# Who makes the two parts of the third query block's weights: POOL alone, or POOL and VectorE

## The chip, the core and the metric

The kernel runs on one core of a Trainium2 chip. The metric is the device time of one execution in microseconds (us); three runs of the kernel before gave 1119.89, 1119.96 and 1120.11, median 1119.96. Every timeline below counts from the start of the profiled span.

## What is computed

An encoder trunk of two layers over 512 tokens of width 1024. Each layer adds a normalised mixer (token attention heads and memory cross-attention heads, then an output projection) and a normalised SwiGLU block. The change sits in the first layer's mixer, in the query projection:

```python
for i in range(DEPTH):
    h = rms_norm(x, g_mix_pre[i])
    proj = h @ w_in[i]
    q = proj[..., :Q_W].reshape(B, S, N_TOK_HEADS, HEAD_DIM)
    ...
    tok = mixer_a(q, k, v, attn_sink[i // N_MIXERS], cos_p, sin_p)
    mo = memory_attention(qm, km, vm)
    o = jnp.concatenate([tok, mo], axis=-1) @ w_o[i]
    x = x + rms_norm(o, g_mix_post[i])
```

`rms_norm(x, g)` multiplies by the vector `g_mix_pre`; the kernel folds that vector into the rows of the weights of the first mixer, so the weights are multiplied by it on their way to TensorE.

## The kernel before

All matrix products are made of 32-bit factors split into a high part `hi` (rounded to TensorE's fp32r format) and a low part `lo`, the remainder; each product is three matmuls, hi by hi, hi by lo, lo by hi (`mm3`, L273 to L275). So every weight block of 128x1024 has to be fetched into a tile `raw`, multiplied by the norm factor where there is one, and split into tiles `whi` and `wlo` before TensorE may use it. There are three `raw` tiles and four of each of `whi` and `wlo`, used in turn, and SP issues the transfers in program order: a transfer waits until the tile that it fills has been read by its last reader.

The first mixer works through a query block of four heads at a time, numbered c = 0 to 3 (c = 3 is the memory heads). Each query block has two weight blocks of 128x1024, z = 0 and 1. In the same stretch of time the mixer makes the keys and values of the memory, and starts the attention of the first heads:

- `prod` and `keys` of the memory (L388 to L427): ScalarE and VectorE take two accumulators in PSUM apart into `k2` and `vm` (L402, L404); POOL copies a part of `k2` (`again`, L414); TensorE turns `k2` twice (L421, L426), and VectorE copies the second result out (`kmb`, L427). The second turn uses one single PSUM bank.
- `score` (L557 to L586): TensorE multiplies queries and keys (L570, L571) into one of three PSUM banks used in turn, VectorE masks and takes the minimum (L576), ScalarE exponentiates (L582). Two of the three banks hold the memory's accumulators before.
- `normalise` (L611): VectorE makes the reciprocal `rd` (L618), POOL multiplies the four tiles `p` of a head by it (L621). `turn` (L624): TensorE transposes `p` (L631).

Who splits a weight block is set by a number per block in the table `PACE`: `qw[2 * c + z]`. It goes as `side` into `unit`, whose inner `part` handles half a block, in columns of 256 (`m`):

```python
            for k in range(c0 // m, c1 // m):
                c = slice(k * m, k * m + m)
                if side & 1:
                    nc.gpsimd.tensor_scalar(raw[:, c], raw[:, c], g[:, k:k + 1], 1.0, op0=OP.mult, op1=OP.mult)
                else:
                    self.split_scaled(hi[:, c], lo[:, c], raw[:, c], g[:, k:k + 1], side)
            if side & 1:
                self.split(hi[:, c0:c1], lo[:, c0:c1], raw[:, c0:c1], side)
```

With 3, POOL scales `raw` in place (L239, 256 columns each), makes `hi` by a multiplication by 1 (L281, 512 columns) and `lo` by a subtraction (L285, 512 columns). With 2, `split_scaled` is used: POOL makes `hi` as `raw` times the factor (L298, 256 columns), and VectorE makes `lo` as `raw` times the factor minus `hi` (L301, 256 columns). The multiplication on VectorE has two tensors in SBUF as sources.

The order on TensorE is written by hand, by times in the table `PACE`; on the other engines a scheduler at build time fixes one order for each, and at run time each engine takes its instructions in that order and waits at the head of its queue.

Of the kernel before, what the change touches and what calls it, by code (L numbers as in the profile page):

```python
# [34 lines left out]
URGENT = 150  # L35
LOTS = ((0, 8), (8, 14), (14, 22))

PACE = [{'lag': 1.692, 'vlag': 0.479, 'jstep': 0.213, 'kstep': 0.375, 'klag': 0.742, 'qoff': [0.212, 0.126, 0.099], 'qlag': 1.02, 'late': 0.6, 'moff': -0.235, 'mdur': 0.562, 'mlag': 0.697, 'kw': [0, 0, 2, 0], 'mw': [2, 1, 1, 0], 'qw': [1, 0, 0, 1, 3, 3, 3, 3], 'hoff': 0, 'ow': [10.3, 10.8, 12.2, 13.2], 'ox': 11.4, 'od': 0.3, 'hstep': 0.872, 'hlag': 1.742, 'hjstep': 0.135, 'hvlag': 0.751, 'owm': [0, 0, 0, 0, 0, 0, 0, 0], 'q0step': 0.27, 'q0off': -0.032, 'q0lag': 0.919, 'm0off': -0.078, 'm0dur': 0.002, 'm0lead': 1.887, 'mlead': 1.201, 'qlead': 0.921, 'q0lead': 1.555, 'qstep': 1.002, 'tw': [0, 0, 0, 0, 0, 0, 0, 0], 'h2off': 0}, {'lag': 1.824, 'vlag': 0.535, 'jstep': 0.218, 'kstep': 0.777, 'klag': 1.715, 'qoff': [-0.027, -0.162, -0.027], 'qlag': 1.189, 'late': 2.15, 'moff': -0.088, 'mdur': 0.384, 'mlag': 1.205, 'kw': [0, 0, 0, 0], 'mw': [0, 0, 0, 0], 'qw': [0, 0, 0, 0, 0, 3, 1, 1], 'hoff': 0, 'ow': [10.2, 10.7, 12.2, 13.2], 'ox': 11.3, 'od': 0.3, 'hstep': 0.946, 'hlag': 1.847, 'hjstep': 0.295, 'hvlag': 0.568, 'owm': [0, 0, 0, 0, 0, 0, 0, 0], 'q0step': 0.718, 'q0off': -0.018, 'q0lag': 1.136, 'm0off': -1.059, 'm0dur': 0.171, 'm0lead': 2.465, 'mlead': 3.162, 'qlead': 1.895, 'q0lead': 1.42, 'qstep': 0.998, 'tw': [0, 0, 0, 0, 0, 0, 0, 0], 'h2off': 0.016}]

# [141 lines left out]
class Trunk:  # L183
# [84 lines left out]
    def side(self, l, key, u):  # L268
        return PACE[l][key][u]

# [400 lines left out]
    def mixer(self, l, mkp, late, tokp):  # L671
        nc = self.nc
        pc = PACE[l]
        if l == 0:
# [619 lines left out]
```

## Time and profile before

| | us |
|---|---|
| median of 3 runs | 1119.96 |
| profiled execution, its own time | 1119.8 |
| its span | 1117.9 |
| TensorE busy | 1095.3 (98% of the span) |
| VectorE (DVE) busy | 838.8 |
| ScalarE (ACT) busy | 662.7 |
| GpSimd (POOL) busy | 202.9 |

The profiled execution lasted 1.9 us longer than its span, and lies 0.16 us below the median. In the rows below PE is TensorE's matmuls, PEld its weight loads, DVE VectorE, ACT ScalarE, POOL GpSimd, SP the engine that issues transfers. A row of a timeline gives start, duration, engine, line, operation, output and inputs, shape, count; in brackets stands how long the engine was idle before, and who ended it.

### The profile page before, as it was taken

How to read it: one execution, taken by the hardware profiler on the slowest of the kernel's cores; microseconds unless marked ns; L12 is line 12 of the kernel's file. 1: busy time of each engine (PE TensorE's matmuls, PEld its weight loads, DVE VectorE, ACT ScalarE, POOL GpSimd, SP SyncE). 2: the span in 40 equal slices, each digit the busy share in tenths (PEclk: the TensorE clock that was granted, in tenths of full speed). 3: DMA queues.
4: the chain of work that ended last, by engine and by line, in shares of the span. 5: the costliest groups of instructions: out<-in, count | busy, mean ns of one | idle time of the engine just before them, and what ended most of it. 6: DMA issues, size and time to landing. Idle time of an engine off the chain costs nothing.

```text
span 1117.9 us, 19566 instructions
## 1 busy us (share of the span) xinstructions
PE 1095.3 (98%) x7487; PEld 1005.7 (90%) x7487; DVE 838.8 (75%) x1401; ACT 662.7 (59%) x1349; POOL 202.9 (18%) x349
## 2 busy tenths in 40 slices
PE   9999999999999999999999999999999999999997
PEld 7889988999889989998898888878999899899986
DVE  5788886899547867885787988758996478669854
ACT  7578984766445544653467888756764256345631
POOL 5693331202000000000343553212000000000001
PEclk9999999999999999999999999999999999999999
DMA  6521025443753382326543221145137123422243
GB/s 238 192 81 50 20 77 188 151 151 116 247 177 108 110 291 76 100 79 209 163 167 114 77 76 39 38 157 183 47 105 226 58 81 113 147 68 98 84 167 113
DMA packets 38686, 139.30 MB, mean 125 GB/s; under 512 B 4416, under 2 KB 4800, under 8 KB 38464
## 3 DMA queue, kind: packets, MB, share of 16 engines
q1 hardware_dynamic: 38448, 137.91, 36.6%
q8 instruction: 59, 0.97, 0.4%
q14 instruction: 35, 0.29, 0.1%
q10 hardware_dynamic: 144, 0.14, 0.0%
HBM read 119.16 MB, written 18.87 MB: 123 GB/s over the span
## 4 chain that ended last, share of the span: by engine, by line
PE 67%; DVE 8%; ACT 3%; POOL 2%; issue 2%; DMA 0%; DVEq 0%; POOLq 0%; ACTq 0%
PE ps L1027 12%; PE ps L1028 11%; PE ps L1026 11%; PE ps L273 9%; PE ps L274 9%; PE ps L275 9%; PE tp L631 2%; PE o L646 1%; PE o L645 1%; DVE wlo L287 1%; DVE sf L287 1%; PE s L570 1%; PE s L571 1%; POOL r L307 1%; ACT junk L311 1%
## 5 line engine op out<-in xcount | busy, mean ns | idle before, releaser
L283 ACT ACTIVATE whi<-raw 128x1024 fp32r<-128x1024 f32 (+2 forms) x186 | 157.9, 863 | 177.9 <-PE ps L1028 78.5
L287 DVE TENSOR_TENSOR wlo<-raw,whi 128x1024 fp32r<-128x1024 f32 (+2 forms) x178 | 175.5, 996 | 74.8 <-ACT whi L283 68.9
L1027 PE MATMUL ps<-sf,wlo 128*128 128x256 f32 x640 | 179.7, 281 | 0.0
L1026 PE MATMUL ps<-sf,whi 128*128 128x256 f32 x640 | 179.7, 281 | 0.0
L1028 PE MATMUL ps<-sf,whi 128*128 128x256 f32 x640 | 179.7, 281 | 0.0
L273 PE MATMUL ps<-whi,f 128*128 128x512 f32 (+1 forms) x360 | 138.6, 385 | 0.0
L274 PE MATMUL ps<-wlo,f 128*128 128x512 f32 (+1 forms) x360 | 138.5, 385 | 0.0
L275 PE MATMUL ps<-whi,f 128*128 128x512 f32 (+1 forms) x360 | 138.4, 384 | 0.0
L1027 PE MATMUL ps<-a,wlo 128*128 128x256 f32 x480 | 134.0, 279 | 1.7 <-DVE wlo L287 1.7
L1026 PE MATMUL ps<-a,whi 128*128 128x256 f32 x480 | 134.4, 280 | 0.3 <-DVE c L1062 0.3
L1028 PE MATMUL ps<-a,whi 128*128 128x256 f32 x480 | 134.4, 280 | 0.0
L1027 PEld LDWEIGHTS ps<-sf,wlo 128*128 128x128 f32 x640 | 121.4, 190 | 0.5
L1026 PEld LDWEIGHTS ps<-sf,whi 128*128 128x128 f32 x640 | 121.1, 189 | 0.5
L1028 PEld LDWEIGHTS ps<-sf,whi 128*128 128x128 f32 x640 | 121.4, 190 | 0.0
L316 POOL TENSOR_SCALAR e<-sso 128x1 f32<-128x1 f32 x8 | 3.4, 422 | 565.5 <-ACT junk L311 565.3
L273 PE MATMUL ps<-whi,hT 128*128 128x256 f32 (+1 forms) x320 | 98.8, 309 | 0.0
L274 PE MATMUL ps<-wlo,hT 128*128 128x256 f32 (+1 forms) x320 | 94.0, 294 | 2.0 <-DVE wlo L287 1.4
L621 POOL TENSOR_SCALAR p<-p,rd 128x256 f32<-128x256 f32 (+2 forms) x128 | 76.9, 619 | 99.7 <-DVE rd L618 41.9
L275 PE MATMUL ps<-whi,hT 128*128 128x256 f32 (+1 forms) x320 | 93.7, 293 | 0.0
L1027 PEld LDWEIGHTS ps<-a,wlo 128*128 128x128 f32 x480 | 90.5, 188 | 2.3 <-DVE wlo L287 2.1
L1026 PEld LDWEIGHTS ps<-a,whi 128*128 128x128 f32 x480 | 90.4, 188 | 0.7 <-DVE c L1062 0.5
L1028 PEld LDWEIGHTS ps<-a,whi 128*128 128x128 f32 x480 | 90.1, 188 | 0.0
(205 smaller groups left out, 2740.3 us busy)
## 6 DMA issues: line engine op xcount, KB each, us to landing
raw<-in_wgu_dram SPq DMA_DIRECT2D x48, 512.0 KB, 4.2
raw<-in_wd_dram SPq DMA_DIRECT2D x44, 512.0 KB, 4.4
rb<-in_wgu_dram SPq DMA_DIRECT2D x40, 512.0 KB, 3.6
raw<-in_wo_dram SPq DMA_DIRECT2D x17, 512.0 KB, 3.6
raw<-in_wq_dram SPq DMA_DIRECT2D x16, 512.0 KB, 4.9
xt<-x SPq DMA_DIRECT2D x12, 512.0 KB, 4.4
raw<-in_wm_dram SPq DMA_DIRECT2D x8, 512.0 KB, 3.9
x<-y SPq DMA_DIRECT2D x8, 512.0 KB, 2.9
```

The costliest lines, as they stand in the source:

```text
L273: mm(out, lh, rh, start=first, stop=False)
L274: mm(out, lh, rl, start=False, stop=False)
L275: mm(out, ll, rh, start=False, stop=last)
L283: a = nc.scalar.activation(hi, src, AF.Copy)
L287: b = nc.vector.tensor_sub(lo, src, hi.bitcast(F32))
L307: g.tensor_tensor(r, r, self.mhalf[:, :r.shape[1]], op=OP.pow)
L311: self.nc.scalar.activation(scratch, x, AF.Square, scale=D ** -0.5, accum_out=ss)
L621: self.pooled = nc.gpsimd.tensor_scalar(hd["p"][z][:, :n], hd["p"][z][:, :n], rd[:, z:z + 1], 1.0, op0=OP.mult, op1=OP.mult)
L631: nc.tensor.transpose(tp[:, z], hd["p"][i][:, jj * P:(jj + 1) * P], self.ident)
L1026: mm(out, wh[:, s], rh, start=start and k == 0, stop=False, skip_group_check=True)
L1027: mm(out, wl[:, s], rh, start=False, stop=False, skip_group_check=True)
L1028: mm(out, wh[:, s], rl, start=False, stop=k == 3, skip_group_check=True)
```

## The change

Two entries of `qw` of the first layer go from 3 to 2, those of query block c = 2, z = 0 and 1. The table is one long line; the two entries are the fifth and sixth:

```diff
-PACE = [{... 'qw': [1, 0, 0, 1, 3, 3, 3, 3], ...
+PACE = [{... 'qw': [1, 0, 0, 1, 2, 2, 3, 3], ...
```

So for `raw_1073` (z = 0) and `raw_1128` (z = 1) the scaling in place, the copy and the subtraction on POOL go; POOL makes `hi` with the factor, VectorE `lo`. The blocks of c = 3, `raw_1579` and `raw_1615`, stay with POOL. The order of TensorE and of SP stays as it is.

POOL, from the split of block c = 1, z = 1 (`raw_705`) to the copy of the memory's second key tile (`k2_833`):

```order
 L285 TENSOR_TENSOR wlo_707<-raw_705,whi_706 128x512 x2
-L281 TENSOR_SCALAR whi_1074<-raw_1073 128x512 x2
-L285 TENSOR_TENSOR wlo_1075<-raw_1073,whi_1074 128x512 x2
-L239 TENSOR_SCALAR raw_1128<-raw_1128,cst_87 128x256 x3
+L298 TENSOR_SCALAR whi_1074<-raw_1073,cst_87 128x256 x4
 L414 TENSOR_SCALAR k2_808<-k2_808 128x4x64
-L239 TENSOR_SCALAR raw_1128<-raw_1128,cst_87 128x256
 L239 TENSOR_SCALAR raw_1579<-raw_1579,cst_87 128x256 x3
-L281 TENSOR_SCALAR whi_1129<-raw_1128 128x512 x2
+L298 TENSOR_SCALAR whi_1129<-raw_1128,cst_87 128x256 x4
 L414 TENSOR_SCALAR k2_833<-k2_833 128x4x64
```

Both before and after, three scalings of `raw_1579` stand ahead of the high part of `raw_1128`; now five instructions lie between the split of `raw_705` and them, where there were nine.

VectorE, from the rotary of the first query block's last tile (`qx_773`) to the memory's keys and values (`k2`, `vm`):

```order
 L437 TENSOR_TENSOR rt_775<-qx_773,cst_87 128x64
 L439 TENSOR_TENSOR qx_773<-qx_773,cst_87 128x4x16
+L301 SCALAR_TENSOR_TENSOR wlo_1075<-raw_1073,cst_87,whi_1074 128x256
 L440 TENSOR_TENSOR qx_773<-qx_773,rt_775 128x4x16
+L301 SCALAR_TENSOR_TENSOR wlo_1075<-raw_1073,cst_87,whi_1074 128x256 x2
 L287 TENSOR_TENSOR q2_791<-qx_773,q2_791 128x4x64
+L301 SCALAR_TENSOR_TENSOR wlo_1075<-raw_1073,cst_87,whi_1074 128x256
 L404 SCALAR_TENSOR_TENSOR k2_808<-ps_551,rs_114,k2_808 128x4x64
 L404 SCALAR_TENSOR_TENSOR vm_550<-ps_551,rs_114,vm_550 128x4x64
+L301 SCALAR_TENSOR_TENSOR wlo_1130<-raw_1128,cst_87,whi_1129 128x256 x3
 L404 SCALAR_TENSOR_TENSOR k2_833<-ps_558,rs_114,k2_833 128x4x64
 L404 SCALAR_TENSOR_TENSOR vm_550<-ps_558,rs_114,vm_550 128x4x64
```

Seven of the eight new subtractions stand ahead of the memory's second key tile, three of them directly ahead of it, and those three read `whi_1129`, which POOL makes.

VectorE, the rows that follow: the first head's masks (L576), the rotary of a tile of query block 1 (`qx_865`), and the copy of the memory's keys (`kmb`):

```order
 L437 TENSOR_TENSOR rt_867<-qx_865,cst_87 128x64
+L301 SCALAR_TENSOR_TENSOR wlo_1130<-raw_1128,cst_87,whi_1129 128x256
 L439 TENSOR_TENSOR qx_865<-qx_865,cst_87 128x4x16
-L440 TENSOR_TENSOR qx_865<-qx_865,rt_867 128x4x16
 L576 ISA p_889,nm_871<-s_886,mask_215,nsink_89 128x384
 L576 ISA nm_871 128x1
-L287 TENSOR_TENSOR q2_892<-qx_865,q2_892 128x4x64
+L440 TENSOR_TENSOR qx_865<-qx_865,rt_867 128x4x16
 L576 ISA p_904,nm_871<-s_901,mask_215,nsink_89 128x384
 L576 ISA nm_871 128x1
+L287 TENSOR_TENSOR q2_892<-qx_865,q2_892 128x4x64
 L427 CAST kmb_549<-tp_913 128x4x128
```

The eighth subtraction joins them, and two steps of the rotary come later; the copy of `kmb` keeps its place behind both masks.

## Rows read from the trace of the kernel before

**Rows 1.** Busy time of each engine, from the page.
```profile
PE 1095.3 (98%) x7487; PEld 1005.7 (90%) x7487; DVE 838.8 (75%) x1401; ACT 662.7 (59%) x1349; POOL 202.9 (18%) x349
```
**Rows 2.** Waits of PE between 40 and 112 us: total, times, longest.
```profile
PE tp L631 <- POOL p L621: 1.3, 2, 1.1
...
PE tp L426 <- DVE kmb L427: 0.3, 1, 0.3
```
**Rows 3.** Timeline of PE, 44 to 112 us.
```profile
65.75 0.45 PE L421 MATMUL tp<-identr,k 128*128 128x128 f32 x4
66.49 0.50 PE L426 MATMUL tp<-identr,k 128*128 128x128 f32 x4 [0.29 <-DVE kmb L427]
...
70.16 0.34 PE L571 MATMUL s<-kb,qT 128*128 128x384 f32 x1
71.56 0.33 PE L631 MATMUL tp<-cst,p 128*128 128x128 f32 x1 [1.06 <-POOL p L621]
72.12 0.33 PE L631 MATMUL tp<-cst,p 128*128 128x128 f32 x1 [0.23 <-POOL p L621]
72.21 0.36 PE L273 MATMUL ps<-whi,hT 128*128 128x256 f32 x1
```
**Rows 4.** Timeline of POOL, 20 to 110 us.
```profile
48.41 3.84 POOL L239 TENSOR_SCALAR raw<-raw,cst 128x256 f32<-128x256 f32 x8 [7.78 <-DMA raw<-in_wq_dram]
54.34 2.54 POOL L285 TENSOR_TENSOR wlo<-raw,whi 128x512 fp32r<-128x512 f32 x2 [2.09 <-ACT whi L283]
56.85 1.21 POOL L281 TENSOR_SCALAR whi<-raw 128x512 fp32r<-128x512 f32 x2
58.03 2.73 POOL L285 TENSOR_TENSOR wlo<-raw,whi 128x512 fp32r<-128x512 f32 x2
60.74 1.39 POOL L239 TENSOR_SCALAR raw<-raw,cst 128x256 f32<-128x256 f32 x3
...
68.53 2.36 POOL L239 TENSOR_SCALAR raw<-raw,cst 128x256 f32<-128x256 f32 x5
70.86 2.23 POOL L621 TENSOR_SCALAR p<-p,rd 128x256 f32<-128x256 f32 x4
```
**Rows 5.** SP's issues, 40 to 44 us; the first of them, us to landing.
```profile
40.66 2.01 SPq L227 DMA_DIRECT2D raw<-in_wq_dram  x2
raw<-in_wq_dram SPq DMA_DIRECT2D x1, 512.0 KB, 7.6
```
**Rows 6.** SP's issue between 56 and 59 us, and its time to landing.
```profile
56.91 0.33 SPq L227 DMA_DIRECT2D raw<-in_wq_dram  x1
raw<-in_wq_dram SPq DMA_DIRECT2D x1, 512.0 KB, 3.9
```
**Rows 7.** Timeline of DVE, 40 to 112 us.
```profile
52.57 1.69 DVE L301 SCALAR_TENSOR_TENSOR wlo<-raw,cst,whi 128x256 fp32r<-128x256 f32 x4 [0.67 <-ACT whi L300]
...
60.95 0.48 DVE L404 SCALAR_TENSOR_TENSOR k<-ps,rs,k 128x256 fp32r<-128x256 f32 x1 [0.56 <-ACT vm L402]
61.35 0.47 DVE L404 SCALAR_TENSOR_TENSOR vm<-ps,rs,vm 128x256 fp32r<-128x256 f32 x1
62.17 0.49 DVE L576 CUSTOM_DVE_ANT_0 p<-s,mask,nsink 128x256 f32<-128x256 f32 x1 [0.35 <-PE s L571]
...
65.66 0.68 DVE L427 CAST kmb<-tp 128x512 fp32r<-128x512 f32 x1
...
68.89 0.17 DVE L618 RECIPROCAL rd<-den 128x4 f32<-128x4 f32 x1
```
**Rows 8.** Four L301 beside POOL: timelines of DVE (26 to 40), POOL (20 to 110).
```profile
34.88 2.01 DVE L301 SCALAR_TENSOR_TENSOR wlo<-raw,cst,whi 128x256 fp32r<-128x256 f32 x4
35.38 2.12 POOL L239 TENSOR_SCALAR raw<-raw,cst 128x512 f32<-128x512 f32 x2 [1.09 <-DMA raw<-in_wm_dram]
```
**Rows 9.** Stretches at the end: engines' busy time, PEclk, DMA share, GB/s.
```profile
1111.00:1112.00 1.00, 0.00 (x0) 0.00 (x0) 0.81 (x2) 0.51 (x2) 0.00 (x0) 1.00 0.72 287
...
1115.00:1116.00 1.00, 0.00 (x0) 0.00 (x0) 0.00 (x0) 0.00 (x0) 0.00 (x0) 0.58 1.00 375
```

More of the change, by code (lines that the diff above doesn't have):

```diff
@@ L36 @@
 LOTS = ((0, 8), (8, 14), (14, 22))
-PACE = [{'lag': 1.692, 'vlag': 0.479, 'jstep': 0.213, 'kstep': 0.375, 'klag': 0.742, 'qoff': [0.212, 0.126, 0.099], 'qlag': 1.02, 'late': 0.6, 'moff': -0.235, 'mdur': 0.562, 'mlag': 0.697, 'kw': [0, 0, 2, 0], 'mw': [2, 1, 1, 0], 'qw': [1, 0, 0, 1, 3, 3, 3, 3], 'hoff': 0, 'ow': [10.3, 10.8, 12.2, 13.2], 'ox': 11.4, 'od': 0.3, 'hstep': 0.872, 'hlag': 1.742, 'hjstep': 0.135, 'hvlag': 0.751, 'owm': [0, 0, 0, 0, 0, 0, 0, 0], 'q0step': 0.27, 'q0off': -0.032, 'q0lag': 0.919, 'm0off': -0.078, 'm0dur': 0.002, 'm0lead': 1.887, 'mlead': 1.201, 'qlead': 0.921, 'q0lead': 1.555, 'qstep': 1.002, 'tw': [0, 0, 0, 0, 0, 0, 0, 0], 'h2off': 0}, {'lag': 1.824, 'vlag': 0.535, 'jstep': 0.218, 'kstep': 0.777, 'klag': 1.715, 'qoff': [-0.027, -0.162, -0.027], 'qlag': 1.189, 'late': 2.15, 'moff': -0.088, 'mdur': 0.384, 'mlag': 1.205, 'kw': [0, 0, 0, 0], 'mw': [0, 0, 0, 0], 'qw': [0, 0, 0, 0, 0, 3, 1, 1], 'hoff': 0, 'ow': [10.2, 10.7, 12.2, 13.2], 'ox': 11.3, 'od': 0.3, 'hstep': 0.946, 'hlag': 1.847, 'hjstep': 0.295, 'hvlag': 0.568, 'owm': [0, 0, 0, 0, 0, 0, 0, 0], 'q0step': 0.718, 'q0off': -0.018, 'q0lag': 1.136, 'm0off': -1.059, 'm0dur': 0.171, 'm0lead': 2.465, 'mlead': 3.162, 'qlead': 1.895, 'q0lead': 1.42, 'qstep': 0.998, 'tw': [0, 0, 0, 0, 0, 0, 0, 0], 'h2off': 0.016}]
@@ new lines @@
+PACE = [{'lag': 1.692, 'vlag': 0.479, 'jstep': 0.213, 'kstep': 0.375, 'klag': 0.742, 'qoff': [0.212, 0.126, 0.099], 'qlag': 1.02, 'late': 0.6, 'moff': -0.235, 'mdur': 0.562, 'mlag': 0.697, 'kw': [0, 0, 2, 0], 'mw': [2, 1, 1, 0], 'qw': [1, 0, 0, 1, 2, 2, 3, 3], 'hoff': 0, 'ow': [10.3, 10.8, 12.2, 13.2], 'ox': 11.4, 'od': 0.3, 'hstep': 0.872, 'hlag': 1.742, 'hjstep': 0.135, 'hvlag': 0.751, 'owm': [0, 0, 0, 0, 0, 0, 0, 0], 'q0step': 0.27, 'q0off': -0.032, 'q0lag': 0.919, 'm0off': -0.078, 'm0dur': 0.002, 'm0lead': 1.887, 'mlead': 1.201, 'qlead': 0.921, 'q0lead': 1.555, 'qstep': 1.002, 'tw': [0, 0, 0, 0, 0, 0, 0, 0], 'h2off': 0}, {'lag': 1.824, 'vlag': 0.535, 'jstep': 0.218, 'kstep': 0.777, 'klag': 1.715, 'qoff': [-0.027, -0.162, -0.027], 'qlag': 1.189, 'late': 2.15, 'moff': -0.088, 'mdur': 0.384, 'mlag': 1.205, 'kw': [0, 0, 0, 0], 'mw': [0, 0, 0, 0], 'qw': [0, 0, 0, 0, 0, 3, 1, 1], 'hoff': 0, 'ow': [10.2, 10.7, 12.2, 13.2], 'ox': 11.3, 'od': 0.3, 'hstep': 0.946, 'hlag': 1.847, 'hjstep': 0.295, 'hvlag': 0.568, 'owm': [0, 0, 0, 0, 0, 0, 0, 0], 'q0step': 0.718, 'q0off': -0.018, 'q0lag': 1.136, 'm0off': -1.059, 'm0dur': 0.171, 'm0lead': 2.465, 'mlead': 3.162, 'qlead': 1.895, 'q0lead': 1.42, 'qstep': 0.998, 'tw': [0, 0, 0, 0, 0, 0, 0, 0], 'h2off': 0.016}]
```

## The prediction

> **What bounds the kernel now.** I read the page's busy times first. TensorE is busy for 1095.3 of the 1117.9 us of the span, the other engines far less [rows 1]: time that TensorE gains or loses in the first mixer arrives at the end nearly one for one, and work that is taken from POOL or given to VectorE counts only where TensorE waits for it. So the second view is TensorE's waits in the stretch of the change, 40 to 112 us. Two of them matter. The largest is for POOL: 1.3 us, for the first head's scaled tiles `p` [rows 2]. The other is 0.3 us for VectorE's copy of `kmb` [rows 2].
>
> The third view is the timelines, for what lies behind each wait. TensorE multiplies the last scores at 70.16 and starts the transposes of `p` only at 71.56, held by POOL; the next product starts at 72.21 [rows 3]. VectorE had the reciprocal ready at 68.89 plus 0.17, that is at 69.06 [rows 7]; but POOL was scaling weights of block c = 3 until 70.89 and took up `p` at 70.86 [rows 4]. So POOL's queue of weights, not the softmax, is what TensorE waits for, and it is that queue which the change shortens. At `kmb`, VectorE is what comes last, 66.49 against a copy started at 65.66 [rows 3, 7]: this is a place where any delay of VectorE goes straight into TensorE.
>
> **What POOL sheds.** For one block before, POOL runs four scalings of 0.48 (3.84 for eight), two copies in 1.21 and two subtractions in 2.73 [rows 4]: 1.92 + 1.21 + 2.73 = 5.9 us. After, it makes four high parts of 256 columns. No such shape of L298 is in the stretch; L239 is the same operation with the same columns, so 0.48 each, 1.92 a block. POOL is relieved of about 4 us a block, 8 in all.
>
> **The gain.** With these 8 us gone POOL has nothing in front of `p` when the reciprocal comes, and TensorE's wait for `p` goes. At least it is the two stated waits, 1.06 + 0.23 = 1.29 us [rows 3]. At most it is all from the end of the scores, 70.16 + 0.34 = 70.50, to the next product at 72.21, 1.71 us [rows 3], as if the two transposes were hidden altogether. I take the middle, **1.5 us**.
>
> **The new wait.** VectorE gets eight L301. Alone four of them took 1.69, 0.42 each [rows 7]; four beside POOL took 2.01, 0.50 each [rows 8]. Were that all, 4 us of additional work would lie in VectorE's queue. But three of them stand directly in front of the memory's second L404, and need the high part of `raw_1128`. POOL makes that behind three scalings of `raw_1579`, and that tile is still on its way:
>
> - The transfer of `raw_1579` fills the tile that `raw_705` leaves. It is issued at 56.91, right after POOL's subtractions of 54.34 to 56.88 [rows 4, 6], which the change does not touch. It lands 3.9 later, at 60.81 [rows 6]. An earlier transfer was issued at 40.66, landed after 7.6, at 48.26, and POOL began at 48.41 [rows 4, 5], so 0.15 more: POOL begins at 60.96. Before, POOL had its own copies and subtractions until 60.74 [rows 4] and never saw this wait; now it is through with its four high parts (56.88 + 1.92 = 58.8) and a short copy, and stands idle for more than a us.
> - Three scalings, 1.39 [rows 4], to 62.35; the first high part, 0.48, at 62.83.
> - VectorE, which is through with its earlier work by about 61, waits there. Three L301 at 0.50, because POOL runs beside them: to 64.33. The L404 that ran at 60.95 [rows 7] runs 3.4 us late.
> - Two L404 at 0.40 (60.95 to 61.35) bring the first mask to 65.13, where it stood at 62.17 after an idle 0.35 [rows 7]: 2.96 late. From there to the copy of `kmb` the same work lies in front as before, plus the eighth L301, 0.50: 2.96 + 0.50 = **3.5 us late**.
> - TensorE waited for that copy already, so its second turn of the keys, at 66.49, comes 3.5 us late as well. Part of that it loses a little earlier, at the third score, whose PSUM bank the second pair of L404 has to free; that is the same delay, not one more.
>
> ScalarE, VectorE and TensorE then go on in step, all of them 3.5 us later. The reciprocal comes at about 72.5, POOL is idle by then and scales two tiles in about 1.1 (four take 2.23 [rows 4]), at 73.6; TensorE arrives at 70.50 + 3.5 = 74.0. So the gain of 1.5 holds, with 0.4 to spare.
>
> SP issues in the same order. The transfer of `raw_1615` hangs on the last L301 of `raw_1073`, at about 60.4, and the first one of the output weights on the last L301 of `raw_1128`, at about 66.7; both have nobody waiting in this stretch. The weights of c = 2 themselves are multiplied many us later, so which engine makes them, and when, is free.
>
> **The price of L301 between POOL's high parts.** The rows give 0.42 alone and 0.50 beside POOL [rows 7, 8], where POOL's two scalings stretched to 2.12 at the same time. The upper bound is that VectorE gets a turn only when one of POOL's instructions has ended: 0.42 + 0.48 = 0.90 each, 1.6 us more over the four that count. I take 0.50, the row of the same shape beside a POOL scaling. By the lower bound the sum is 0.3 smaller. The Trainium skill (GPSIMD Engine Reference, Specifications) says that POOL shares its SBUF interfaces with VectorE, with contention where VectorE's instruction has two SBUF inputs, which L301 has. Taken at its strictest it gives the upper bound, and the trace agrees with it as to the sign, 0.50 against 0.42, but not as to full exclusion.
>
> **The sum.** 3.5 - 1.5 = +2.0 us. The profiled execution took 1119.8, so 1121.8; it lies 0.16 under the median of the runs, so the forecast of a median is **1122.0**, 0.18% above. What a measurement can tell from no change is about 0.2%, 2.24 us or 1122.2: the forecast lies just inside it. The bounds give its own range: 0.3 less for L301 and 0.2 for the gain, 1121.5, to 1.6 and 0.2 more, 1123.8.
>
> **The rivals.**
>
> - *POOL and VectorE take turns (slower).* Each of the four L301 that count waits for one of POOL's instructions; +2.0 + 1.6 = +3.6, 1123.6. For it: POOL's scalings in rows 8 were stretched, so they do get in each other's way. It is decided by L301's duration: from 0.56 on, the time passes 1122.2. Against full turns: 0.50. It takes in that the reciprocal is so late that 0.4 us of margin is gone and TensorE waits for `p` again.
> - *VectorE does not wait (not slower).* If POOL's high part of `raw_1128` were ready when VectorE comes to it, only L301's own work is left, seven at 0.42 to 0.50 in front of the copy, of which VectorE's idle time and POOL's missing subtractions pay much; TensorE would keep the gain, -1.5, or lose about as much as it gains: 1118.5 to 1120.0. It needs a landing before 59.5; the transfer is issued at 56.91, and 3.9 speaks against it [rows 6].
> - *The clock falls in the longer stalls.* TensorE would stand still for some 1.4 and 2.4 us close together. In the trace it is granted full speed in all slices in which it works; at the end it stands still from 1111 on at 1.00, and falls only in the slice from 1115, to 0.58 [rows 9]. So 4 us of rest cost nothing there. If it fell to half for as long as the stalls last, about 3.5 us, half of that would be lost: +1.7, 1123.7. The Trainium skill (TensorE: Matmul & The Clock Gate, Part 1) says that a long enough rest brings 1.2 GHz and sustained work 2.4 GHz again; the trace agrees as to the fall, and no row shows a rise.
>
> **How the numbers follow.** The forecast's case has 0.70, turns 0.13, no wait 0.12, the clock 0.05. Within the forecast's case somewhat more than half of the chance lies under 1122.2 (0.40 against 0.30). Faster by over 2.24 us asks for more than the whole gain: 0.03, out of the case without a wait, whose other 0.09 is no change. No change within 0.2%: 0.40 + 0.09 = 0.49. Slower: 0.30 + 0.13 + 0.05 = 0.48. The range takes the forecast's case, the turns, the clock and the dearer half of no wait: 1120.0 to 1124.0.
>
> **What would show it.** POOL idle for about 1 to 2 us ahead of the scaling at 61.0, released by the transfer; VectorE idle before an L301 until 62.8, released by L298; TensorE held at L570 and L426 by VectorE, 3 us or more together, until about 70; no wait of L631 for POOL between 70 and 76; PEclk at 1.00. It is wrong if VectorE has no idle time ahead of L301 beyond 1 us, if L631 still waits for POOL, or if TensorE's order after 76 us is not shifted by one and the same 2 us.

## The result, and the profile after

| | us |
|---|---|
| changed kernel, median of 22 runs | 1121.22 (1120.33 to 1123.27) |
| kernel before, median of 22 runs beside them | 1119.69 (1118.90 to 1120.38) |
| ratio of the two | 1.0016, 95% interval 1.0010 to 1.0022 |
| profiled execution, its own time and span | 1121.31, 1119.2 (before 1119.8, 1117.9) |

The change makes the kernel slower by 0.16%. That is less than the 0.2% which the prediction took for no change, but the interval does not contain 1. Measured a second time (the run `after_again` below) the ratio was 1.0017 (1.0008 to 1.0026).

The page of the profiled execution, busy time of each engine, in the order of [rows 1]:

```profile
PE 1095.6 (98%) x7487; PEld 1005.7 (90%) x7487; DVE 840.3 (75%) x1409; ACT 662.0 (59%) x1349; POOL 196.5 (18%) x341
```

POOL lost 6.4 us and eight instructions, VectorE got 1.5 us and eight instructions, TensorE has the same work. None of that is the result; it lies in what TensorE waits for. PE's waits between 40 and 112 us (total, times, longest), against [rows 2]:

```profile
PE s L570 <- DVE vm L404: 1.5, 1, 1.5
PE tp L426 <- DVE kmb L427: 1.4, 1, 1.4
```

The wait of L631 for POOL is gone; what other waits are left are of 0.2 us. In its place TensorE waits for VectorE twice, 2.9 us together. The granted clock (PEclk) is 1.00 in every us from 62 to 76 of this trace, as in the trace of the kernel before, so the clock has no part in these waits. The timeline of POOL in the changed kernel shows how both come about:

```profile
57.09 2.23 POOL L298 TENSOR_SCALAR whi<-raw,cst 128x256 fp32r<-128x256 f32 x4
59.40 0.46 POOL L414 TENSOR_SCALAR k<-k 128x256 fp32r<-128x256 f32 x1
60.91 1.39 POOL L239 TENSOR_SCALAR raw<-raw,cst 128x256 f32<-128x256 f32 x3 [1.05 <-DMA raw<-in_wq_dram]
62.27 2.18 POOL L298 TENSOR_SCALAR whi<-raw,cst 128x256 fp32r<-128x256 f32 x4
...
71.91 2.30 POOL L621 TENSOR_SCALAR p<-p,rd 128x256 f32<-128x256 f32 x4 [4.39 <-DVE rt L437]
```

POOL is through at 59.86, stands idle for 1.05 us for the transfer of `raw_1579`, and makes the high part of `raw_1128` (the second L298) only behind three scalings of that tile. Later it is idle for 4.39 us before `p`, where in [rows 4] it went from weights to `p` without a pause. On the timeline of DVE in the same kernel the three L301 ahead of the second L404 wait for that high part, and all that follows is late:

```profile
62.80 1.93 DVE L301 SCALAR_TENSOR_TENSOR wlo<-raw,cst,whi 128x256 fp32r<-128x256 f32 x3 [1.48 <-POOL whi L298]
64.64 0.47 DVE L404 SCALAR_TENSOR_TENSOR k<-ps,rs,k 128x256 fp32r<-128x256 f32 x1
...
65.43 0.47 DVE L576 CUSTOM_DVE_ANT_0 p<-s,mask,nsink 128x256 f32<-128x256 f32 x1
...
68.76 0.68 DVE L427 CAST kmb<-tp 128x512 fp32r<-128x512 f32 x1
...
71.57 0.17 DVE L618 RECIPROCAL rd<-den 128x4 f32<-128x4 f32 x1
```

And the timeline of PE, against [rows 3]:

```profile
62.92 0.34 PE L570 MATMUL s<-ka,qT 128*128 128x384 f32 x1
...
65.65 0.41 PE L570 MATMUL s<-ka,qT 128*128 128x384 f32 x1 [1.51 <-DVE vm L404]
...
69.59 0.51 PE L426 MATMUL tp<-identr,k 128*128 128x128 f32 x4 [1.37 <-DVE kmb L427]
...
73.28 0.34 PE L571 MATMUL s<-kb,qT 128*128 128x384 f32 x1
73.46 0.38 PE L631 MATMUL tp<-cst,p 128*128 128x128 f32 x2
73.60 0.36 PE L273 MATMUL ps<-whi,hT 128*128 128x256 f32 x1
...
77.20 0.46 PE L546 MATMUL tp<-identr,q 128*128 128x128 f32 x4
```

The row at 62.92 stood at 62.69 before the change, so this execution came to the place 0.23 us later. Against that, L426 is 69.59 - 66.49 - 0.23 = 2.87 us late. From L426 to the product behind the transposes it now takes 73.60 - 69.59 = 4.01 us, where it took 72.21 - 66.49 = 5.72 [rows 3]: 1.71 us are won. The sum is 2.87 - 1.71 + 0.23 = 1.39. The last of these rows shows it: it stands 1.40 later than in the kernel before, where it was

```profile
75.80 0.46 PE L546 MATMUL tp<-identr,q 128*128 128x128 f32 x4
```

The medians differ by 1.53 and the spans of the two traces by 1.3. That the spans agree so well with 1.39 is partly chance, since the two traces differ in two more places. The kernel before waits for VectorE at 346.33 (L1062, 0.33 us), the changed kernel does not, and the matmuls behind that place are only 0.74 later; between 790 and 865 us the shift grows again to 1.32. Whether either belongs to the change was not tried.

### The profile page after: what moved, and what is told of

Same layout as the page of the kernel before. It is cut to its first block, busy times and chain, and to the rows that moved or that the text cites. A ratio compares the mean times of both kernels' runs of the same rounds, so it can differ in the third digit from the quotient of the medians.

```text
span 1119.2 us, 19571 instructions
## 1 busy us (share of the span) xinstructions
PE 1095.6 (98%) x7487; PEld 1005.7 (90%) x7487; DVE 840.3 (75%) x1409; ACT 662.0 (59%) x1349; POOL 196.5 (18%) x341
## 4 chain that ended last, share of the span: by engine, by line
PE 68%; DVE 7%; ACT 2%; POOL 2%; issue 2%; DVEq 0%; POOLq 0%; ACTq 0%
PE ps L1027 12%; PE ps L1028 12%; PE ps L1026 12%; PE ps L274 9%; PE ps L273 9%; PE ps L275 9%; PE tp L631 2%; PE o L646 1%; DVE sf L287 1%; DVE wlo L287 1%; PE o L645 1%; PE s L570 1%; PE s L571 1%; POOL r L307 1%; DVE a L287 1%
## 5 line engine op out<-in xcount | busy, mean ns | idle before, releaser
L287 DVE TENSOR_TENSOR wlo<-raw,whi 128x1024 fp32r<-128x1024 f32 (+2 forms) x178 | 175.5, 996 | 75.3 <-ACT whi L283 72.4
```

The lines of the kernel that those rows point to most:

```text
L287: b = nc.vector.tensor_sub(lo, src, hi.bitcast(F32))
```

## The experiments

The two theories. **The wait in the queue**: the cost is that VectorE stands at an L301 whose high part is late, with the memory's keys and values and the masks behind it. **The work**: the cost is L301 itself on VectorE beside POOL. In the diffs, `issue_after(x)` makes the scheduler place an instruction behind `x`; it changes no value. The kernel before took 1119.35 in the median beside the first four runs, and 1119.23 beside the last three.

### The four L301 of `raw_1128` placed behind the copy of `kmb` (`lo_behind`)

```diff
 def keys(...)
-        nc.vector.tensor_copy(kb[:, :, c], tp[:, :n])
+        self.lastkey = nc.vector.tensor_copy(kb[:, :, c], tp[:, :n]).ins
 def split_scaled(..., after=None)
-        nc.vector.scalar_tensor_tensor(lo, src, r, ...)
+        with (self.tc.issue_after(after) if after else nullcontext()): nc.vector.scalar_tensor_tensor(lo, src, r, ...)
 # after = self.lastkey for the block (l, c, z) == (0, 2, 1), None elsewhere
```

> The changed kernel, with one edit: the four L301 of raw_1128 (z = 1) are ordered on VectorE behind the copy of the memory's second keys (kmb). POOL's work and order stay those of the change. Theory (VectorE waits for POOL's high part of raw_1128 in front of the memory's L404, and that delay goes through kmb into TensorE): no idle of VectorE ahead of the second L404, TensorE's waits at L570 and L426 (1.5 and 1.4 us in the change) gone, the wait of L631 for POOL stays gone or comes back with at most 0.5 us, since one L301 now lies ahead of the reciprocal; 1.2 to 1.9 us under the kernel before, 1117.8 to 1118.5, and 2.7 to 3.4 under the change. Rival A (the cost is the work of eight L301 on VectorE and its interference with POOL, wherever it stands): within 0.5 us of the change, 1120.7 to 1121.7. Rival B (the clock falls in the change and that is the cost): the time falls only as far as the clock of the runs rises, and TensorE's waits stay.

Measured: 1117.95 (1117.45 to 1119.47), ratio to before 0.9988 (0.9979 to 0.9997), span 1115.8. POOL's order is that of the changed kernel, with its idle 1.09 us for the transfer. On DVE's timeline the three L301 that waited are gone from the place ahead of the second L404 (a wait of 0.41 us for POOL at 57.49, for the first L301 of `raw_1073`, stays, as in the changed kernel), and the copy of `kmb` starts where it did in [rows 7]:

```profile
61.11 0.47 DVE L404 SCALAR_TENSOR_TENSOR k<-ps,rs,k 128x256 fp32r<-128x256 f32 x1
...
65.58 0.68 DVE L427 CAST kmb<-tp 128x512 fp32r<-128x512 f32 x1
...
67.55 0.47 DVE L301 SCALAR_TENSOR_TENSOR wlo<-raw,cst,whi 128x256 fp32r<-128x256 f32 x1
67.95 0.16 DVE L617 TENSOR_TENSOR den<-den,es 128x4 f32<-128x4 f32 x1
```

PE's waits for L570 and L426 are gone, that of L631 for POOL too. With the same work on every engine, the order of four instructions on VectorE turns +1.5 into -1.4. The gain of an unburdened POOL is real, and this is about its size: 1119.35 - 1117.95 = 1.40. The clock does not explain it either: TensorE's waits went, and the mean clocks of these runs, 0.998 and 0.999, are those of the kernel before.

### POOL's high parts of `raw_1128` placed ahead of the scalings of `raw_1579` (`hi_first`)

```diff
-                    nc.gpsimd.tensor_scalar(raw[:, c], raw[:, c], g[:, k:k + 1], 1.0, ...)
+                    with (self.tc.issue_after(self.lasthi) if late else nullcontext()): nc.gpsimd.tensor_scalar(raw[:, c], ...)
 def split_scaled(...)
-            nc.gpsimd.tensor_scalar(hi, src, r, 1.0, op0=OP.mult, op1=OP.mult)
+            self.lasthi = nc.gpsimd.tensor_scalar(hi, src, r, 1.0, op0=OP.mult, op1=OP.mult).ins
 # late for the block (l, c, z) == (0, 3, 0) alone
```

> The changed kernel, with one edit: POOL makes the four high parts of raw_1128 ahead of the scalings of raw_1579, so it does not wait for that transfer first. VectorE's three L301 still stand in front of the memory's second L404, the fourth in front of the first mask. Theory: the high parts start when the first key copy is done, about 59.9 instead of 62.3; VectorE's idle of 1.48 us ahead of L301 goes, its L301 work stays: kmb about 0.9 us later than before instead of 2.9, with the gain of 1.7 kept: 0.8 us under the kernel before, 1118.5 to 1119.4. Rival A (the work of L301, not the wait): within 0.5 us of the change. If the three scalings and the transfer were not the cause, TensorE's waits at L570 and L426 would stay near 1.5 and 1.4.

Measured: 1118.71 (1118.13 to 1119.54), ratio 0.9995 (0.9986 to 1.0003). The interval takes in 1, so this is not told apart from the kernel before. Here VectorE keeps the L301 ahead of `kmb`, but does not wait for POOL at the three of `raw_1128`, and TensorE's wait at L570 is gone; PE's waits, and two rows of DVE's timeline:

```profile
PE tp L426 <- DVE kmb L427: 1.3, 1, 1.3
```

```profile
60.86 1.63 DVE L301 SCALAR_TENSOR_TENSOR wlo<-raw,cst,whi 128x256 fp32r<-128x256 f32 x3
...
66.51 0.68 DVE L427 CAST kmb<-tp 128x512 fp32r<-128x512 f32 x1
```

This takes the two theories apart. The work of four L301 ahead of `kmb` delays its copy from 65.58 to 66.51, by 1.2 us if one counts that this execution came to L570 0.25 us earlier (62.55 against 62.80), and the medians differ by 1118.71 - 1117.95 = 0.76. Waiting for POOL's late high part costs the rest: this kernel lies 0.64 below the one before, the changed kernel 1.53 above, 2.2 between them. Both theories have a part; the wait has three quarters, the falls of the clock that come with it (below) included.

### Only one of the two blocks given to VectorE (`z0only`, `z1only`)

```diff
-'qw': [1, 0, 0, 1, 2, 2, 3, 3]
+'qw': [1, 0, 0, 1, 2, 3, 3, 3]    # z0only
+'qw': [1, 0, 0, 1, 3, 2, 3, 3]    # z1only
```

> Half of the change: only raw_1073 (z = 0) goes to POOL's high part and VectorE's low part, raw_1128 is split by POOL alone as before. Theory: the four L301 that VectorE gets do not wait long and are paid by its idle time; no new wait at L570; POOL reaches the first tile p at about 69.4 instead of 70.9, so most of the wait of L631 goes: 1.0 to 1.7 us under the kernel before, 1118.0 to 1118.7. Rival A (each L301 costs the same): half of the change's cost, about 1120.4.

> The other half: only raw_1128 (z = 1) is changed, raw_1073 is split by POOL alone as before. Theory: VectorE waits for the high part as in the change; POOL comes to it about 0.5 us later, since the copies and subtractions of raw_1073 now lie where it waited for the transfer. The wait of L631 for POOL is gone as in the change. 0 to 0.8 us above the change, 1121.2 to 1122.0. Rival A: half of the change's cost, about 1120.4.

`z0only`: 1117.85 (1117.32 to 1118.70), ratio 0.9987 (0.9978 to 0.9995). The four L301 of `raw_1073` fit in ahead of the memory's keys, and the copy of `kmb` starts at 65.57. POOL still splits `raw_1128`, but with one block less it is nearly in time for `p` (its row, and PE's wait):

```profile
69.78 2.21 POOL L621 TENSOR_SCALAR p<-p,rd 128x256 f32<-128x256 f32 x4
```

```profile
PE tp L631 <- POOL p L621: 0.2, 1, 0.2
```

So half of the change gives all of the gain. `z1only`: 1121.36 (1120.37 to 1123.11), ratio 1.0018 (1.0009 to 1.0026), as slow as the whole change. POOL never waits for the transfer there, since its own work, the copies and subtractions of `raw_1073` and a key copy, lasts until 61.5; the high part of `raw_1128` is late all the same, and VectorE stands idle for it (row of DVE's timeline):

```profile
63.35 1.92 DVE L301 SCALAR_TENSOR_TENSOR wlo<-raw,cst,whi 128x256 fp32r<-128x256 f32 x3 [2.60 <-POOL whi L298]
```

TensorE waits 2.0 us at L570 there (this trace is of an execution of 1122.83, in which the clock fell as well, see below). So what costs is that these L301 stand in this place with a late input; what makes the input late, the transfer and three scalings in the change or POOL's own work here, is the same to TensorE.

### The changed kernel again, and with POOL's high part later still (`after_again`, `longer4`)

```diff
-                    self.split_scaled(hi[:, c], ...)
+                    [nc.gpsimd.tensor_scalar(raw[:, :512], raw[:, :512], 1.0, 1.0, op0=OP.mult, op1=OP.mult) for _ in range(4 if late and k == 0 else 0)]; self.split_scaled(hi[:, c], ...)
 # longer4; late for the block (l, c, z) == (0, 2, 1) alone
```

> The changed kernel once more, unaltered, beside the next one on the same chip. Both theories: 1121.2 in the median (1120.3 to 1122), 1.3 to 1.6 above the kernel before, with two or three executions in eleven between 1122.9 and 1123.3 at a mean clock of 0.996 to 0.997, as in 4 of the 22 runs so far. If no execution lies above 1122.5, the fall of the clock belongs to particular chips, not to the length of TensorE's stall alone.

> The changed kernel with four multiplications by 1 added on POOL, in place, of 512 columns of raw_1128 each, ahead of its high part (they change no value). The order on VectorE and TensorE stays. Two of them, 0.62 each like the copies of L281, end before the transfer of raw_1579 has landed and fill POOL's idle 1.05 us; of the rest, some 1.2 us, and the 0.3 that the idle time does not cover, the first high part should come 0.4 to 0.9 us later. Theory of the wait in the queue: the three L301 ahead of the second L404 of the memory, that L404 and the turn of the keys come later by the same 0.4 to 0.9, VectorE's idle time before L301 grows to 1.9 to 2.4, and the time goes to 1121.6 to 1122.1, plus more executions at 1122.9 and above, so that the median itself may lie at 1122 to 1123.5. Rival, that the cost is L301's own work on VectorE beside POOL: the three L301 last about as long as before, and the time stays within 0.3 of the changed kernel's.

`after_again`: 1121.17 (1120.36 to 1123.34). `longer4`: 1121.64 (1120.67 to 1122.90), ratio 1.0020 (1.0011 to 1.0029). In the trace of `longer4` POOL has no idle time left ahead of the scalings, and the high part follows the last multiplication by 1. The scheduler also put two of the three scalings of `raw_1579` behind the high part, so that it waits for one of them and not for three:

```profile
61.45 0.48 POOL L239 TENSOR_SCALAR raw<-raw,cst 128x256 f32<-128x256 f32 x1
61.89 0.62 POOL L241 TENSOR_SCALAR raw<-raw 128x512 f32<-128x512 f32 x1
62.49 2.17 POOL L298 TENSOR_SCALAR whi<-raw,cst 128x256 fp32r<-128x256 f32 x4
```

```profile
PE s L570 <- DVE vm L404: 2.2, 1, 2.2
```

TensorE's wait at L570 grew from 1.5 to 2.2, the median by 0.4 to 0.5: the sign of the queue's theory, and the low end of its size. But the runs of either kernel spread over more than 2 us. Resampled from the runs, the 95% interval of the difference to the 33 of the changed kernel reaches from -0.6 to +1.6, so the times prove nothing here; the longer wait in the trace supports the theory. VectorE's idle time ahead of L301 was 1.60, short of the 1.9 expected: its L404 of the first tile ran at 60.94, 0.1 later than in the changed kernel, while TensorE was half a us earlier.

The trace of `after_again` happens to be of an execution of 1123.2, and shows what two traced long executions have in common, this one and that of `z1only` (1122.83). Stretches of that trace: length, busy time of PE, PEld, DVE, ACT and POOL, PEclk, DMA share, GB/s:

```profile
64.00:66.00 2.00, 0.45 (x4) 0.24 (x3) 2.00 (x5) 0.00 (x0) 2.00 (x5) 1.00 0.00 0
...
67.00:68.00 1.00, 1.00 (x10) 1.00 (x9) 1.00 (x6) 0.17 (x2) 0.98 (x2) 0.75 0.00 0
68.00:69.00 1.00, 1.00 (x8) 1.00 (x7) 0.70 (x4) 1.00 (x4) 0.00 (x0) 0.50 0.77 201
...
73.00:74.00 1.00, 1.00 (x8) 1.00 (x7) 0.93 (x6) 0.60 (x2) 0.61 (x2) 0.50 0.00 0
74.00:75.00 1.00, 1.00 (x8) 1.00 (x8) 0.15 (x2) 0.61 (x2) 1.00 (x2) 0.84 0.00 0
75.00:76.00 1.00, 1.00 (x10) 0.97 (x9) 0.90 (x4) 0.77 (x2) 0.52 (x2) 1.00 0.00 0
```

TensorE stands still for 1.7 us at L570, works again from 66.12, and from about 67.5 to 74.3 it is granted half speed, 1.2 GHz in place of 2.4. In the trace of `z1only` TensorE stands still for 1.95 us, and the half speed lasts from about 67.5 to 74.3 too. The same stretch of the changed kernel's own trace, with a standstill of 1.5 us:

```profile
64.00:66.00 2.00, 0.49 (x4) 0.38 (x3) 2.00 (x8) 0.06 (x1) 2.00 (x5) 1.00 0.00 0
66.00:68.00 2.00, 2.00 (x22) 1.96 (x20) 2.00 (x7) 1.18 (x5) 1.52 (x3) 1.00 0.23 29
68.00:70.00 2.00, 0.63 (x8) 0.51 (x6) 1.56 (x6) 2.00 (x7) 0.00 (x0) 1.00 0.62 234
```

No fall here, and yet the waits of 1.5 and 1.4 us: the change costs its 1.5 us without a fall, and a fall comes on top. Between 1122.8 and 1123.4 lie 4 of 22 and 3 of 11 executions of the changed kernel, 2 of 11 of `z1only`, 3 of 11 of `longer4`; all have a mean clock of 0.996 or 0.997. The converse does not hold: 3 more of `after_again`, 4 of `z1only` and 6 of `longer4` have such a clock and took between 1120.37 and 1122.49, so a lower mean clock alone does not make an execution long. None of the 33 executions of `lo_behind`, `hi_first` and `z0only` lies above 1119.6, nor has any a mean clock under 0.998; of the 26 of the kernel before beside the last three, one has 0.997 (1121.03). In the trace of `longer4` the fall was short (0.71 at 66 to 67, 0.50 until 69, 0.58 until 70, then 1.00), and that execution took about 1120.7. No wait at L426 is left in that trace, so the slower matmuls filled a time in which TensorE would have waited for VectorE anyway. For the other short executions with a lower clock no trace shows where it fell.

### All eight new L301 behind the copy of `kmb` (`lo_behind_both`)

The edit is that of `lo_behind`, with `after` for both blocks of c = 2.

> The changed kernel with all eight new L301 (both blocks) ordered on VectorE behind the copy of kmb, not only the four of raw_1128. Theory of the wait in the queue: with four of them behind the copy there was no wait left at L570 and L426, so the other four have nothing more to give: 1117.5 to 1118.2, like the kernel with four behind (1117.95). If L301's own work ahead of kmb still cost something, it would be faster than that by more than 0.5. A danger on the other side: the transfer of raw_1615 starts only when the last L301 of raw_1073 has read its tile, some 8 us later, and the weights of the output projection after it; if anything waits for those, TensorE gets a new wait after 75 us and the time passes 1118.5.

Measured: 1121.15 (1119.99 to 1122.47), ratio 1.0017 (1.0008 to 1.0026). The forecast missed by three us, and the danger that it named came true, by way of POOL's queue. The waits at L570 and L426 are gone; a new one stands at 86.80. PE's row, and POOL's rows ahead of it:

```profile
86.80 1.04 PE L631 MATMUL tp<-cst,p 128*128 128x128 f32 x2 [3.05 <-POOL p L621]
```

```profile
76.51 2.28 POOL L239 TENSOR_SCALAR raw<-raw,cst 128x256 f32<-128x256 f32 x4
...
83.61 2.67 POOL L285 TENSOR_TENSOR wlo<-raw,whi 128x512 fp32r<-128x512 f32 x2
86.27 2.05 POOL L621 TENSOR_SCALAR p<-p,rd 128x256 f32<-128x256 f32 x4
```

The L301 of `raw_1073` read their tile late, so the transfer of `raw_1615`, which fills that tile, came between 71.5 and 75.1 us; POOL's scaling of it began at 76.51, and its whole split stands in front of the third head's `p`. The weights of `raw_1615` have nobody waiting, but POOL's queue has. From 87 to 92 us the granted clock was 0.50, so the clock fell there as well, and all 11 executions have a mean clock of 0.995 to 0.997. TensorE's L546 came 2.36 us earlier than in the kernel before at 73.44 (75.80 there) and 3.18 later at 93.06 (89.88): 5.5 us lost, of which the wait is 3.05. Most of the rest lies in the stretch at half clock; the two were not tried apart.

## Why the prediction was right, and where its sizes were off

It put the time at 1122.0 within 1120.0 to 1124.0, 0.18% above the kernel before, and 1121.22 came out, 0.16% above; the sign and the mechanism were right, the cost of the mechanism was 0.6 too large and its gain 0.2 too small. Some of the nearness is luck. The terms of the cost were off in both directions and cancel in part, and of the 0.78 between forecast and median 0.27 lies in the base, since 1119.96 of three runs became 1119.69 of 22; as a difference, 2.0 was said and 1.53 came.

- **The gain.** Said: 1.5, at most 1.71. In the trace 1.71, so the two transposes are hidden altogether, the upper bound. The margin of 0.4 held: POOL's second tile is ready at about 71.91 + 1.15 = 73.06, TensorE comes at 73.46. In runs, `lo_behind` and `z0only` lie 1.4 and 1.5 below the kernel before.
- **What POOL sheds.** Said: 8 us. POOL's busy time fell by 6.4; the eight high parts took 2.23 + 2.18 = 4.41 instead of 3.84. This did no harm, with POOL idle for 4.39 ahead of `p`.
- **POOL's wait for the transfer.** Said: idle for more than a us, begins at 60.96, first high part at 62.83, VectorE idle until then. Measured: idle 1.05, begins at 60.91, VectorE begins L301 at 62.80. The transfer landed after 3.6 us, not 3.9; with the start 0.23 later, the two nearly cancel.
- **The price of L301.** Said: 0.50 each, for the three 1.50. Measured: 62.80 to 64.64, 1.84, 0.61 each; POOL's L298 beside them took 2.18 for four, 0.55 each, where `lo_behind` shows 1.84, 0.46 each, with nothing of this kind on VectorE. In `lo_behind`, an L301 with POOL idle took 0.40. In `hi_first` three L301 beside L298 took 1.55, 0.52 each, so the price is not a fixed one. In the sum this term was 0.34 too small. The row that it came from [rows 8] was of L301 beside L239, not beside L298. The Trainium skill (GPSIMD Engine Reference, Specifications) says that the two engines contend for SBUF where VectorE has two inputs there: the trace agrees that both are slowed, here by half on VectorE and a fifth on POOL, and neither is shut out.
- **From the first mask to the copy of `kmb`.** Said: the same work as before plus one L301, 3.49 + 0.50 = 3.99. Measured: 65.43 to 68.76, 3.33, though the L301 is there and took 0.62. This is **the largest miss of the sum**, 0.66. The prediction took the rows between the two as fixed work, and they were not. In the kernel before they are, on DVE's timeline:

```profile
62.59 0.45 DVE L437 TENSOR_TENSOR rt<-qx,cst 128x64 f32<-128x64 f32 x1
63.07 0.42 DVE L439 TENSOR_TENSOR qx<-qx,cst 128x64 f32<-128x64 f32 x1
63.53 0.42 DVE L440 TENSOR_TENSOR qx<-qx,rt 128x64 f32<-128x64 f32 x1
...
64.49 0.71 DVE L287 TENSOR_TENSOR q<-qx,q 128x256 fp32r<-128x256 f32 x1
```

and in the changed kernel

```profile
65.83 0.21 DVE L437 TENSOR_TENSOR rt<-qx,cst 128x64 f32<-128x64 f32 x1
65.97 0.70 DVE L301 SCALAR_TENSOR_TENSOR wlo<-raw,cst,whi 128x256 fp32r<-128x256 f32 x1
66.59 0.21 DVE L439 TENSOR_TENSOR qx<-qx,cst 128x64 f32<-128x64 f32 x1
...
67.26 0.33 DVE L440 TENSOR_TENSOR qx<-qx,rt 128x64 f32<-128x64 f32 x1
...
68.42 0.43 DVE L287 TENSOR_TENSOR q<-qx,q 128x256 fp32r<-128x256 f32 x1 [0.29 <-ACT q L283]
```

  Summed by durations, the four took 2.00 before and 1.18 now. Why the small ones are shorter was not tried. They have another instruction between them now, where L437, L439 and L440 stood directly one behind the other. POOL's work beside them is hardly the reason for these three, since it runs the same scalings in both kernels, in the kernel before and in the changed one:

```profile
62.49 1.85 POOL L239 TENSOR_SCALAR raw<-raw,cst 128x256 f32<-128x256 f32 x4
```

```profile
64.96 2.56 POOL L239 TENSOR_SCALAR raw<-raw,cst 128x256 f32<-128x256 f32 x5
```

  Beside L287 POOL worked before (L281) and is idle now. The page shows the same on the whole: by the starts on the timeline the eight new L301 take 0.62 + 1.16 + 0.40 + 1.84 + 0.62 = 4.64 us, and VectorE's busy time grew by 1.5.
- **The sum.** 0.26 earlier at the first L301 (62.80 - 0.23 against 62.83), 0.34 more for L301, 0.66 less up to `kmb`: 3.46 - 0.26 + 0.34 - 0.66 = 2.88, the 2.87 of the trace. Less the gain of 1.71 and plus the 0.23 of this execution's start, 1.39 against the 2.0 said.
- **The rivals.** *Turns*: it named 0.56 for L301 as the point that decides, and L301 took 0.61; the median still stayed below 1122.2, since the cheaper rotary steps paid for it. Full turns, 0.90, did not happen. *VectorE does not wait*: it idled for 1.48. *The clock falls*: given 0.05, and too low: 10 of the 33 executions of the changed kernel have a mean clock of 0.996 or 0.997, and 7 of them are long. The price was close for these, 1.7 said, and the seven lie 1.7 to 2.2 above the median. The prediction had reasoned from a stall at the end [rows 9] that 4 us of rest cost nothing; the runs refute that as a rule. The Trainium skill (TensorE: Matmul & The Clock Gate, Part 1) says that the point at which the clock goes over to the higher level varies from run to run of one kernel. No run here was made to show that; what varies between two traces of one kernel here is whether the clock falls at all.
- **The signs.** Met: POOL's idle time, VectorE's idle time, no wait of L631 for POOL. Nearly met: TensorE held at L570 and L426 for 2.9 us, where 3 or more were said. PEclk was 1.00 in this trace, not in every execution. Not met as written: TensorE's order after 76 us should have shifted by one and the same 2 us; it shifted by 1.40, then 0.74, then 1.3.

## What to carry to other kernels

Giving the queue of an engine with idle time an instruction means giving it that instruction's wait: read which late input it has, and what stands behind it. Here the right question was not whether VectorE has time for eight L301, but whether the three ahead of the memory's keys have their input; with four of them moved back, or only the block with an early input given to VectorE, the change is a gain of 0.12% or 0.13% in place of a loss of 0.16%. Moving back too many breaks the next thing, a tile that is freed late, and the price is paid 20 us further on, where another engine's queue holds TensorE up.

## What the runs showed of the hardware that was not expected

Almost the same standstill of TensorE, 1.5 and 1.7 us at L570, left the granted clock at 1.00 in one execution of a kernel and halved it for nearly 7 us in another, starting more than a us after TensorE was at work again. In `longer4`, behind a standstill of 2.2 us, the fall came about half a us after it and lasted some 3 us. What decides between the two was not settled by these runs. And L301 on VectorE and L298 on POOL, each 128x256 and side by side, slow each other: from 0.40 to 0.61 and from 0.46 to 0.55 us in the changed kernel, and to 0.52 and 0.63 in `hi_first` (POOL's partly beside L404), with neither shut out while the other works.
